# A transformer block pair with a product-key expert layer: order, pacing and engines of the row gathers and of the gate tables' one-hots

## The chip, the cores and the metric
One core of a Trainium2 chip runs the whole kernel. The metric is the device time of one execution in microseconds; the median of several runs is given. TensorE (PE in the profile, its weight loads PEld), VectorE (DVE), ScalarE (ACT), GpSimd (POOL) and SyncE (SP, which here only starts DMAs) each work through their own list of instructions in order and wait on semaphores.

## The reference
256 tokens of width 1024 go through two attention layers with feed-forward parts, a token mixer, a cross attention, and at the end an expert layer (`peer`). Only that last layer bears on the change:

```python
q = (xt @ w_pq).reshape(T, 8, 2, 128)
s = einsum('thpd,hpnd->thpn', q, subkeys)        # 2 x 128 scores per head
...                                              # top 16 of 128 twice, top 16 of their 256 sums
gate = softmax(best_s)                           # 8 heads x 16 experts per token
act = gelu(einsum('thkd,td->thk', peer_u[expert], xb)) * gate
out = einsum('thk,thkd->td', act, peer_v[expert])
```

`peer_u` and `peer_v` are tables of 16384 rows (128 x 128) of 1024 floats. Each token picks 128 rows of each.

## The kernel before
`phase_peer` splits the tokens. The first 192 (`TD`) are worked out **densely** on TensorE: all 16384 activations are formed, column by column (128 columns `j` of 128 experts), and multiplied with a gate table that is nearly all zeros. The last 64 tokens (`TS`) are worked out by **gathering** their rows: with two halves of the picks on the 128 partitions there are 64 indirect transfers of 128 rows from the `u` table and 64 from the `v` table, 512 KB each.

- **Column loop u** (L1589 to L1607): `whole` brings 512 KB of `u` per column in one of ten buffers, eight float32 matmuls make the column's scores (L1593, two TensorE instructions each in the trace), `ev_u` (L1537) applies Gelu on ScalarE (L1541, L1544) and, for tokens whose gate table is there already, multiplies it in on VectorE (L1542). In the first 71 columns the top-16 routing of both token groups is spread over the columns. `gather` (L1391) ends a group's routing and writes the transposed picks into the tables `IT`, `JT`, `GT` (L1417 to L1419).
- **Gate tables** (`gates`, L1514): from column `J0` = 75 on, `pump` (L1549) spreads 192 tokens over the matmuls. A token's 128 x 128 gate table is the product of two one-hot matrices (L1526): `oi` (`onehot`, L1500, four tokens at a time; three of the four on ScalarE as Abs and Relu, L1504 and L1505, the fourth on VectorE, L1506), made a group of four ahead, and `oj` times the gate (`weighed`, L1509, VectorE, L1511), made three tokens ahead in four buffers. After four tokens VectorE multiplies the table into the finished columns of `A` (L1531) and ScalarE copies the rest (L1533).
- **Column loop v** (L1639): `column` (L1620) brings 512 KB of `v` per column. Seven of eight columns are split into `hi` and `lo` parts (`granule`, L204: ScalarE L211, VectorE L212; `raw` has four buffers, `hi` and `lo` three each), as is the column of `A` (`split`, L268, L270 and L271), and cost 16 TensorE instructions (L1636, L1637); every eighth is used whole in float32 (L1634), also 16 instructions. Loop v adds up into eight PSUM banks. The last four columns stand apart (L1652) so that the final normalisation can start bank by bank.
- **Rows** (`gathered`, L1428): a generator that starts one transfer on GpSimd's queue per step (L1451). `beat[0]` is the newest column matmul; the transfer gets a semaphore wait on it. A transfer's use (`take`, L1433) is emitted when three later transfers have been started: for `u` VectorE multiplies with the token and adds up (L1438), for `v` it adds the row times its weight into `sacc` (L1446). `row` has four buffers. `Pace` (L1556) hands out the steps: 80 over the last 116 columns of loop u, 54 over 110 columns of loop v (L1586, L1587). `take` has no order of its own towards TensorE.

All instructions are emitted in Python's order, and the framework orders each engine's list from that by priority and by when operands and buffers come free; `granule` gives the split of a `v` column a lead of 80 instructions (L210, L1291). A dependency of class `Sync` is a semaphore wait on the chip; one of class `NoSync` only puts an instruction behind another when the lists are made.

Of the kernel before, what the change touches and what calls it, by code (L numbers as in the profile page):

```python
# [9 lines left out]
F32 = mybir.dt.float32  # L10
# [4 lines left out]
AF = mybir.ActivationFunctionType  # L15
OP = mybir.AluOpType
# [1269 lines left out]
def phase_peer(k, pool, wpool, out):  # L1286

    nc, I = k.nc, k.I
    mm = nc.tensor.matmul
    V = nc.vector  # L1290
    k.lead = 80  # L1291
    TS = 64
    TD = T - TS
# [18 lines left out]
    def slot(n, w):  # L1312
        return slots[:, n * 256:n * 256 + w]

    iota = wpool.tile([128, 128], F32, name="iota", bufs=1)
    nc.sync.dma_start(iota, I["consts"][:, CCOL["iota"]:CCOL["iota"] + 128])
    IT = wpool.tile([128, TD], F32, name="IT", bufs=1)
    JT = wpool.tile([128, TD], F32, name="JT", bufs=1)
    GT = wpool.tile([128, TD], F32, name="GT", bufs=1)

    es = wpool.tile([128, 64], I32, name="es", bufs=1)
    gs = wpool.tile([128, 64], F32, name="gs", bufs=1)
    hs = wpool.tile([128, 64], F32, name="hs", bufs=1)
    ws = wpool.tile([128, 64], F32, name="ws", bufs=1)
    x2 = wpool.tile([128, D], F32, name="x2", bufs=1)
# [65 lines left out]
    def gather(tt):  # L1391
        ri, rj, bv = picks[tt]

        mx = k.small.tile([128, 8], F32, name="pmx", bufs=2)
        V.tensor_reduce(mx, bv, AX.X, OP.max)
        V.tensor_tensor(bv, bv, mx[:, :, None].to_broadcast([128, 8, 16]), OP.subtract)
        nc.scalar.activation(bv, bv, AF.Exp)
        V.tensor_reduce(mx, bv, AX.X, OP.add)
        rc = k.small.tile([128, 8], F32, name="prc", bufs=2)
        V.reciprocal(rc, mx)  # L1400
        V.tensor_tensor(bv, bv, rc[:, :, None].to_broadcast([128, 8, 16]), OP.mult)
        ri, rj, bv = (t.rearrange("p a r -> p (a r)") for t in (ri, rj, bv))
        if tt == 1:

            own = slice(S0, 128)
            e = slot(8, 64).bitcast(I32)
            V.scalar_tensor_tensor(e[own], ri[own, 0:64], 128.0, rj[own, 0:64], op0=OP.mult, op1=OP.add)
            V.scalar_tensor_tensor(es[own], ri[own, 64:128], 128.0, rj[own, 64:128], op0=OP.mult, op1=OP.add)
            nc.sync.dma_start(es[0:S0], e[own])
            nc.sync.dma_start(gs[0:S0], bv[own, 0:64])  # L1410
            nc.sync.dma_start(gs[own], bv[own, 64:128])
        ps = k.tp()
        for n, src in enumerate((ri, rj, bv)):
            nc.tensor.transpose(ps[:, n * 128:n * 128 + 128], src, k.ident)
        w = min(128, TD - tt * 128)
        s = slice(tt * 128, tt * 128 + w)
        V.tensor_scalar(IT[:, s], ps[:, 0:w], -1.0, None, op0=OP.mult)  # L1417
        V.tensor_copy(JT[:, s], ps[:, 128:128 + w])
        V.tensor_copy(GT[:, s], ps[:, 256:256 + w])  # L1419
        yield  # L1420

    def routing(tt):
        for h in range(0, 8, 2):
            yield from interleave([route(h + i, tt) for i in range(2)])
        yield from gather(tt)


    def gathered():  # L1428
        AHEAD = 3
        todo = []  # L1430
        sacc = None

        def take():  # L1433
            nonlocal sacc
            kind, c, r = todo.pop(0)
            col = slice(c, c + 1)
            if kind == "u":
                V.scalar_tensor_tensor(r, r, 1.0, x2, op0=OP.mult, op1=OP.mult, accum_out=hs[:, col])  # L1438
                if c == 63:
                    nc.scalar.activation(ws, hs, AF.Gelu)  # L1440
                    V.tensor_tensor(ws, ws, gs, OP.mult)
            elif c == 0:
                sacc = wpool.tile([128, D], F32, name="x2", bufs=1)
                V.tensor_scalar(sacc, r, ws[:, col], None, op0=OP.mult)
            else:
                V.scalar_tensor_tensor(sacc, r, ws[:, col], sacc, op0=OP.mult, op1=OP.add)  # L1446

        for kind, table in (("u", urow), ("v", vrow)):
            for c in range(64):
                r = wpool.tile([128, D], F32, name="row", bufs=4)  # L1450
                i = nc.gpsimd.indirect_dma_start(out=r, out_offset=None, in_=table,  # L1451
                                                 in_offset=bass.IndirectOffsetOnAxis(ap=es[:, c:c + 1], axis=0))

                k.tc.add_manual_dep(i.ins, beat[0].ins.name, mybir.DependencyInfo(
                    mybir.DependencyClass.Sync, mybir.DependencyReason.DATA), reason="pace")
                todo.append((kind, c, r))
                if len(todo) > AHEAD:
                    take()
                yield
        while todo:  # L1460
            take()
            yield
        low = wpool.tile([128, D], F32, name="row", bufs=4)
        nc.sync.dma_start(low[S0:128], sacc[0:S0])
        x = k.x[S0:128, 1, :]
        V.tensor_tensor(x, x, sacc[S0:128], OP.add)
        yield
        V.tensor_tensor(x, x, low[S0:128], OP.add)
        yield

    J0 = 75
# [13 lines left out]
    def whole(j, ap):  # L1485

        name, bufs = (("raw", 4), ("hi", 3), ("raw", 4), ("lo", 3))[j % 4]
        raw = k.ring.tile([128, 1024], F32, name=name, bufs=bufs)
        nc.sync.dma_start(raw, ap)
        return raw  # L1490

    beat = [None]
# [7 lines left out]
    def onehot(t0):  # L1500

        oi = wpool.tile([128, 4, 128], F32, name="oi", bufs=2)
        for u in range(3):
            nc.scalar.activation(oi[:, u], iota, AF.Abs, bias=IT[:, t0 + u:t0 + u + 1])  # L1504
        nc.scalar.activation(oi[:, 0:3], oi[:, 0:3], AF.Relu, bias=k.one_col, scale=-1.0)  # L1505
        V.tensor_scalar(oi[:, 3], iota, IT[:, t0 + 3:t0 + 4], 0.0, op0=OP.add, op1=OP.is_equal)  # L1506
        return oi

    def weighed(t):  # L1509
        oj = wpool.tile([128, 128], F32, name="oj", bufs=4)  # L1510
        V.tensor_scalar(oj, iota, JT[:, t:t + 1], GT[:, t:t + 1], op0=OP.is_equal, op1=OP.mult)  # L1511
        return oj

    def gates():  # L1514
# [22 lines left out]
    def ev_u(j, ps):  # L1537
        n = done
        if n:
            g = wpool.tile([128, TD], F32, name="ge", bufs=2)  # L1540
            nc.scalar.activation(g[:, :n], ps[:, :n], AF.Gelu)  # L1541
            V.tensor_tensor(A[:, j, :n], A[:, j, :n], g[:, :n], OP.mult)  # L1542
        if n < TD:
            nc.scalar.activation(A[:, j, n:], ps[:, n:], AF.Gelu)  # L1544
# [4 lines left out]
    def pump():  # L1549
        nonlocal slot_no, emitted  # L1550
        slot_no += 1
        while emitted < TD * slot_no / (8 * (128 - J0) - 16):
            next(tables, None)
            emitted += 1
# [18 lines left out]
    for c in range(8):  # L1573
        ps = k.tp()
        nc.tensor.transpose(ps[:, 0:128], xn[0][:, c * 128:c * 128 + 128], k.ident)
        nc.tensor.transpose(ps[:, 128:TD], xn[1][0:S0, c * 128:c * 128 + 128], k.ident[0:S0, 0:S0])
        col = k.gains[:, GCOL["peer"] + c:GCOL["peer"] + c + 1]
# [5 lines left out]
    FIRST = 12  # L1583
    routes = [Pace(early, 16, FIRST), Pace(late, 29, J0 - 4 - FIRST)]
    rows = gathered()
    rows_u = Pace(rows, 80, 128 - FIRST)  # L1586
    rows_v = Pace(rows, 54, 110)  # L1587

    for j in range(128):  # L1589
        w = whole(j, I["u"][j])  # L1590
        ps = k.acc()
        for c in range(8):
            beat[0] = mm(ps[:, :TD], w[:, c * 128:c * 128 + 128], xf[:, c], start=c == 0, stop=c == 7)  # L1593
            if j >= J0:
                pump()
        ev_u(j, ps[:, :TD])
        cols = j + 1
        if j < FIRST:
            routes[0]()
        elif j < J0 - 4:  # L1600
            routes[1]()
        if j == FIRST - 1:
            routes[0].rest()
        if j == J0 - 5:
            routes[1].rest()
        if j >= FIRST:
            rows_u()  # L1607
    for _ in tables:
        pass

# [72 lines left out]
    s = k.small.tile([128, 2], F32, name="ss", bufs=2)  # L1683
    V.tensor_tensor(s, ss[:, 0], ss[:, 1], OP.add)
    inv = k.rsqrt(s, 2, 1.0 / D)
    for tt in range(2):
        nc.scalar.activation(y[:, tt, 0:512], z[:, tt, 0:512], AF.Copy, scale=inv[:, tt:tt + 1])
        V.tensor_scalar(y[:, tt, 512:1024], z[:, tt, 512:1024], inv[:, tt:tt + 1], None, op0=OP.mult)
        for nb in range(2):
            n = slice(nb * 512, nb * 512 + 512)  # L1690
# [3 lines left out]
def body(tc, I, out, upto=None):  # L1694
# [6 lines left out]
    with ExitStack() as root:  # L1701
# [25 lines left out]
        if "peer" in todo:  # L1727
            with ExitStack() as c:
                phase_peer(k, *pools(c, "peer", "p", "w"), out)
        else:  # L1730
            for tt in range(2):
                nc.sync.dma_start(out[0, tt * 128:tt * 128 + 128, :], k.x[:, tt, :])
# [15 lines left out]
```

## Time and profile before

| | us |
|---|---|
| median of 3 runs (lowest, highest) | 1837.44 (1831.9, 1841.64) |
| the profiled execution | 1830.55 |
| its span, first to last instruction | 1828.8 |
| TensorE busy in the span | 1757.9 (96%) |
| VectorE / ScalarE busy | 1213.9 (66%) / 871.9 (48%) |

The columns of loop u run from about 1061 us to 1458 us of the span, with gate tables from about 1267 us; loop v follows to about 1815 us. Busy time of TensorE is that of overlapping instructions, so a stretch at 100% can be at its peak or not; where the pace matters, instructions per microsecond are counted. The sum of the prediction is made against the 1830.55 us of the profiled execution.

### The profile page before, as it was taken

The numbers are of one execution on the slowest core, as the hardware profiler recorded it, in microseconds if no ns is written. First come the engines' busy times: TensorE is split into PE (matmuls) and PEld (weight loads), VectorE is DVE, ScalarE is ACT, GpSimd is POOL, SyncE is SP. The second block draws the span as 40 slices with busy tenths as digits, with TensorE's granted clock in tenths as the row PEclk, the third lists the DMA queues.
The fourth block names the chain that finished last, engine by engine and source line by source line (L and its number), as shares of the span: only waits on it lengthen the run. The fifth ranks groups of instructions, "written<-read, shape, count | busy, mean of one in ns | idle before, by whom it ended". The sixth has DMA issues, their size and how long they took to land.

```text
span 1828.8 us, 30479 instructions
## 1 busy us (share of the span) xinstructions
PE 1757.9 (96%) x11606; PEld 1642.5 (90%) x11606; DVE 1213.9 (66%) x2486; ACT 871.9 (48%) x1737; POOL 192.1 (11%) x184
## 2 busy tenths in 40 slices
PE   8999999999999999999999999999999988888897
PEld 7889998888899879988788999999999888888897
DVE  6867675688677566744475886775677766666665
ACT  6655544555544457765454521113555534343443
POOL 2000000000000001220000002222111122211200
PEclk9999999999999999999999999999999999999999
DMA  7435555643565656322463478999777688787864
GB/s 243 124 121 184 179 184 191 191 133 108 174 183 184 189 192 197 127 92 81 151 214 121 162 241 308 326 336 326 243 236 234 199 274 281 269 282 265 289 220 137
DMA packets 105363, 374.47 MB, mean 205 GB/s; under 512 B 12385, under 2 KB 14081, under 8 KB 104833
## 3 DMA queue, kind: packets, MB, share of 16 engines
q1 hardware_dynamic: 86080, 303.31, 50.8%
q0 software_dynamic: 19136, 69.21, 10.6%
q8 instruction: 92, 1.51, 0.3%
q14 instruction: 55, 0.44, 0.1%
HBM read 368.20 MB, written 3.15 MB: 203 GB/s over the span
## 4 chain that ended last, share of the span: by engine, by line
PE 69%; issue 14%; DMA 7%; DVE 5%; POOL 2%; ACT 2%; POOLq 0%; SPq 0%; ACTq 0%; DVEq 0%
PE acc L217 15%; PE acc L219 15%; PE acc L218 14%; PE acc L1593 13%; DMA row<-in_v,es 4%; DMA row<-in_urow,es 3%; POOL row L1451 2%; DVE lo L212 2%; PE tp L1144 1%; PE tp L1526 1%; ACT hi L211 1%; PE tp L395 1%; PE tp L325 1%; PE tp L407 1%; PE tp L402 1%
## 5 line engine op out<-in xcount | busy, mean ns | idle before, releaser
L211 ACT CAST hi<-raw 128x1024 fp32r<-128x1024 f32 (+2 forms) x420 | 436.4, 1039 | 562.8 <-PE acc L219 159.4
L212 DVE TENSOR_TENSOR lo<-raw,hi 128x1024 fp32r<-128x1024 f32 (+2 forms) x420 | 512.7, 1221 | 247.5 <-ACT hi L211 243.7
L217 PE MATMUL acc<-xal,hi 128*128 128x256 f32 x1272 | 365.6, 287 | 0.8 <-ACT hi L211 0.8
L219 PE MATMUL acc<-xah,lo 128*128 128x256 f32 x1272 | 361.7, 285 | 0.5 <-DVE lo L212 0.5
L218 PE MATMUL acc<-xah,hi 128*128 128x256 f32 x1272 | 361.8, 285 | 0.0
L217 PEld LDWEIGHTS acc<-xal,hi 128*128 128x128 f32 x1272 | 244.8, 192 | 2.8 <-ACT hi L211 1.2
L219 PEld LDWEIGHTS acc<-xah,lo 128*128 128x128 f32 x1272 | 244.5, 192 | 1.2 <-DVE lo L212 0.8
L218 PEld LDWEIGHTS acc<-xah,hi 128*128 128x128 f32 x1272 | 244.9, 193 | 0.6 <-issue 0.2
L1593 PE MATMUL acc<-xf,raw 128*128 128x192 f32 x1024 | 193.3, 328 | 0.0
L1593 PEld LDWEIGHTS acc<-xf,raw 128*128 128x128 f32 x1024 | 167.4, 192 | 0.1
L1446 DVE SCALAR_TENSOR_TENSOR x<-row,ws,x 128x1024 f32<-128x1024 f32 x63 | 80.8, 1283 | 99.9 <-DMA row<-in_v,es 99.9
L1438 DVE SCALAR_TENSOR_TENSOR row<-row,x 128x1024 f32<-128x1024 f32 x64 | 78.2, 1221 | 85.6 <-DMA row<-in_urow,es 85.4
L1451 POOL DMA_INDIRECT row<-in_v,es x64 | 70.9, 1108 | 288.1 <-PE acc L1637 150.7
L1593 PE MATMUL acc<-xf,hi 128*128 128x192 f32 x512 | 96.4, 327 | 0.0
L1451 POOL DMA_INDIRECT row<-in_urow,es x64 | 65.3, 1020 | 296.4 <-PE tp L1360 88.9
L1593 PE MATMUL acc<-xf,lo 128*128 128x192 f32 x512 | 95.8, 327 | 0.0
L1544 ACT ACTIVATE A<-acc 128x192 f32<-128x192 f32 (+25 forms) x125 | 36.8, 298 | 113.4 <-PE acc L1593 112.9
L1526 PE MATMUL tp<-oj,oi 128*128 128x128 f32 x384 | 76.1, 280 | 10.7 <-DVE oj L1511 9.9
L1636 PE MATMUL tp<-xah,hi 128*128 128x384 f32 x252 | 83.1, 379 | 0.0
L1593 PEld LDWEIGHTS acc<-xf,hi 128*128 128x128 f32 x512 | 82.9, 191 | 0.1
L1593 PEld LDWEIGHTS acc<-xf,lo 128*128 128x128 f32 x512 | 82.8, 191 | 0.1
L1526 PEld LDWEIGHTS tp<-oj,oi 128*128 128x128 f32 x384 | 66.2, 190 | 16.8 <-DVE oj L1511 12.1
(477 smaller groups left out, 3574.1 us busy)
## 6 DMA issues: line engine op xcount, KB each, us to landing
raw<-in_v SPq DMA_DIRECT2D x128, 512.0 KB, 4.7
raw<-in_u SPq DMA_DIRECT2D x64, 512.0 KB, 4.8
raw<-in_gate SPq DMA_DIRECT2D x44, 512.0 KB, 3.6
raw<-in_up SPq DMA_DIRECT2D x44, 512.0 KB, 3.6
raw<-in_down SPq DMA_DIRECT2D x44, 512.0 KB, 3.6
hi<-in_u SPq DMA_DIRECT2D x32, 512.0 KB, 4.7
lo<-in_u SPq DMA_DIRECT2D x32, 512.0 KB, 5.1
raw<-in_gates SPq DMA_DIRECT2D x16, 512.0 KB, 3.5
```

The costliest lines, as they stand in the source:

```text
L211: nc.scalar.copy(hi[:, :w], raw[:, :w])
L212: nc.vector.tensor_tensor(lo[:, :w], raw[:, :w], hi.bitcast(F32)[:, :w], OP.subtract)
L217: mm(ps, ah, bl, start=start, stop=False)
L218: mm(ps, ah, bh, start=False, stop=False)
L219: mm(ps, al, bh, start=False, stop=stop)
L1438: V.scalar_tensor_tensor(r, r, 1.0, x2, op0=OP.mult, op1=OP.mult, accum_out=hs[:, col])
L1446: V.scalar_tensor_tensor(sacc, r, ws[:, col], sacc, op0=OP.mult, op1=OP.add)
L1451: i = nc.gpsimd.indirect_dma_start(out=r, out_offset=None, in_=table, in_offset=bass.IndirectOffsetOnAxis(ap=es[:, c:c + 1], axis=0))
L1526: mm(ps[:, u * 128:u * 128 + 128], oi[:, u], ojs.pop(0), start=True, stop=True)
L1544: nc.scalar.activation(A[:, j, n:], ps[:, n:], AF.Gelu)
L1593: beat[0] = mm(ps[:, :TD], w[:, c * 128:c * 128 + 128], xf[:, c], start=c == 0, stop=c == 7)
L1636: mm(acc[c][:, 0:2 * TD], vh[:, s], m, start=j == 0, stop=False)
```

## The change
Rows: a use of a row gets a `NoSync` dependency on `beat[0]`, the column matmul that is newest when the third later transfer is started; the transfer keeps its `Sync` dependency (a helper, `behind`, makes both). Pacing: 38 steps over columns 12 to 74 and 48 over columns 75 to 127 of loop u, 48 over 112 columns of loop v. One-hots: `oi` of four tokens is one VectorE comparison of 128 x 512; three of four `oj` are made by ScalarE in two instructions (Abs, then Relu with the gate as bias and its negative as scale), every fourth by VectorE as before. `gather` writes `IT` without a sign, and by ScalarE the negatives `NJT` and `NGT`.

```diff
-        V.tensor_scalar(IT[:, s], ps[:, 0:w], -1.0, None, op0=OP.mult)
-        V.tensor_copy(JT[:, s], ps[:, 128:128 + w])
-        V.tensor_copy(GT[:, s], ps[:, 256:256 + w])
+        for n, (t, m) in enumerate(((IT, None), (JT, NJT), (GT, NGT))):
+            V.tensor_copy(t[:, s], ps[:, n * 128:n * 128 + w])
+            if m is not None:
+                nc.scalar.activation(m[:, s], ps[:, n * 128:n * 128 + w], AF.Copy, scale=-1.0)
...
+        def behind(i, how):
+            k.tc.add_manual_dep(i.ins, beat[0].ins.name, mybir.DependencyInfo(how, mybir.DependencyReason.DATA),
+                                reason="pace")
...
             if kind == "u":
-                V.scalar_tensor_tensor(r, r, 1.0, x2, op0=OP.mult, op1=OP.mult, accum_out=hs[:, col])
-                if c == 63:
-                    nc.scalar.activation(ws, hs, AF.Gelu)
-                    V.tensor_tensor(ws, ws, gs, OP.mult)
+                i = V.scalar_tensor_tensor(r, r, 1.0, x2, op0=OP.mult, op1=OP.mult, accum_out=hs[:, col])
...
+            behind(i, mybir.DependencyClass.NoSync)
+            if (kind, c) == ("u", 63):
+                nc.scalar.activation(ws, hs, AF.Gelu)
+                V.tensor_tensor(ws, ws, gs, OP.mult)
...
-                k.tc.add_manual_dep(i.ins, beat[0].ins.name, mybir.DependencyInfo(
-                    mybir.DependencyClass.Sync, mybir.DependencyReason.DATA), reason="pace")
+                behind(i, mybir.DependencyClass.Sync)
...
         oi = wpool.tile([128, 4, 128], F32, name="oi", bufs=2)
-        for u in range(3):
-            nc.scalar.activation(oi[:, u], iota, AF.Abs, bias=IT[:, t0 + u:t0 + u + 1])
-        nc.scalar.activation(oi[:, 0:3], oi[:, 0:3], AF.Relu, bias=k.one_col, scale=-1.0)
-        V.tensor_scalar(oi[:, 3], iota, IT[:, t0 + 3:t0 + 4], 0.0, op0=OP.add, op1=OP.is_equal)
+        V.tensor_tensor(oi, iota[:, None, :].to_broadcast([128, 4, 128]),
+                        IT[:, t0:t0 + 4, None].to_broadcast([128, 4, 128]), OP.is_equal)
         return oi
...
-        V.tensor_scalar(oj, iota, JT[:, t:t + 1], GT[:, t:t + 1], op0=OP.is_equal, op1=OP.mult)
+        if t % 4 == 0:
+            V.tensor_scalar(oj, iota, JT[:, t:t + 1], GT[:, t:t + 1], op0=OP.is_equal, op1=OP.mult)
+        else:
+            nc.scalar.activation(oj, iota, AF.Abs, bias=NJT[:, t:t + 1])
+            nc.scalar.activation(oj, oj, AF.Relu, bias=GT[:, t:t + 1], scale=NGT[:, t:t + 1])
         return oj
...
-    rows_u = Pace(rows, 80, 128 - FIRST)
-    rows_v = Pace(rows, 54, 110)
+    rows_early = Pace(rows, 38, J0 - FIRST)
+    rows_late = Pace(rows, 48, 128 - J0)
+    rows_v = Pace(rows, 48, 112)
...
-        if j >= FIRST:
-            rows_u()
+        if j >= J0:
+            rows_late()
+        elif j >= FIRST:
+            rows_early()
```

## Rows read from the trace of the kernel before

**Rows 1.** Page: busy us (share of the span) xinstructions by engine
```profile
PE 1757.9 (96%) x11606; PEld 1642.5 (90%) x11606; DVE 1213.9 (66%) x2486; ACT 871.9 (48%) x1737; POOL 192.1 (11%) x184
```

**Rows 2.** Windows, us: PE, PEld, DVE, ACT, POOL busy (instructions), clock, DMA share, GB/s
```profile
1250.00:1458.00 208.00, 197.25 (x1304) 191.14 (x1303) 145.07 (x410) 104.51 (x349) 38.17 (x39) 1.00 0.71 239
1458.00:1740.00 282.00, 248.24 (x1593) 242.14 (x1592) 186.26 (x233) 114.40 (x185) 57.09 (x50) 0.96 0.81 278
```

**Rows 3.** Windows of 20 us: a full one of loop u, one disturbed and one full of loop v
```profile
1220.00:1240.00 20.00, 20.00 (x125) 20.00 (x125) 17.54 (x56) 5.35 (x13) 5.60 (x5) 1.00 0.93 342
...
1580.00:1600.00 20.00, 18.51 (x106) 18.26 (x107) 12.40 (x16) 5.19 (x8) 3.78 (x3) 0.83 0.61 201
...
1780.00:1800.00 20.00, 20.00 (x141) 20.00 (x139) 10.92 (x13) 9.04 (x13) 0.00 (x0) 1.00 0.69 223
```

**Rows 4.** Waits (us in total, times, longest), 1458 to 1740
```profile
PEld tp L1637 <- DVE lo L212: 39.7, 23, 4.0
...
DVE x L1446 <- DMA row<-in_v,es: 86.3, 37, 6.6
...
ACT hi L211 <- DMA raw<-in_v: 87.8, 39, 4.5
```

**Rows 5.** Chain that ended last, one round of it in loop v
```profile
1494.87 7.28 DMA row<-in_v,es
...
1503.45 1.23 DVE lo L212
```

**Rows 6.** Tile row, whole span, then tile raw, 1470 to 1735
```profile
DMA to landing us min/median/max: 4.1/5.9/9.0
...
DMA to landing us min/median/max: 3.4/4.9/8.7
```

**Rows 7.** Groups by line, 1560 to 1829: VectorE and ScalarE work of a loop v column
```profile
L212 DVE TENSOR_TENSOR lo<-raw,hi 128x1024 fp32r<-128x1024 f32 x80 | 97.6, 1221 | 32.2 <-ACT hi L211 32.2
L211 ACT CAST hi<-raw 128x1024 fp32r<-128x1024 f32 x79 | 82.8, 1049 | 147.5 <-PE acc L1636 68.5 <-DMA raw<-in_v 50.6 <-DVE x L1446 11.9
L1446 DVE SCALAR_TENSOR_TENSOR x<-row,ws,x 128x1024 f32<-128x1024 f32 x32 | 41.0, 1282 | 58.8 <-DMA row<-in_v,es 58.8
L271 DVE TENSOR_TENSOR xah<-A,xah 128x192 fp32r<-128x192 f32 x42 | 14.7, 351 | 0.0
```

**Rows 8.** Waits, 1250 to 1458: weight loads and VectorE
```profile
PEld tp L1526 <- DVE oj L1511: 12.1, 17, 1.8
...
DVE row L1438 <- DMA row<-in_urow,es: 39.1, 25, 4.5
DVE x L1446 <- DMA row<-in_v,es: 13.6, 10, 2.9
```

**Rows 9.** Timeline: one token's two instructions, four of the column's, the next token's
```profile
1301.87 0.39 PE L1526 MATMUL tp<-oj,oi 128*128 128x128 f32 x2
...
1302.09 0.82 PE L1593 MATMUL acc<-xf,raw 128*128 128x192 f32 x4
...
1302.74 0.38 PE L1526 MATMUL tp<-oj,oi 128*128 128x128 f32 x2
```

**Rows 10.** Groups by line, 1267 to 1458 (last row: 1000 to 1100)
```profile
L1511 DVE TENSOR_SCALAR oj<-iota,JT,GT 128x128 f32<-128x128 f32 x188 | 57.6, 347 | 4.5 <-PE tp L1526 4.1
L1506 DVE TENSOR_SCALAR oi<-iota,IT 128x128 f32<-128x128 f32 x46 | 13.0, 282 | 0.0
L1531 DVE TENSOR_TENSOR A<-A,tp 128x300 f32<-128x300 f32 (+46 forms) x47 | 26.5, 563 | 2.6 <-PE tp L1526 1.8 <-issue 0.5
...
L1504 ACT ACTIVATE oi<-iota,IT 128x128 f32<-128x128 f32 x138 | 46.6, 393 | 29.9 <-PE tp L1526 29.9
L1505 ACT ACTIVATE oi<-oi,one_col 128x384 f32<-128x384 f32 x46 | 28.3, 616 | 0.7
L1533 ACT COPY A<-tp 128x212 f32<-128x212 f32 (+46 forms) x47 | 11.8, 250 | 45.5 <-DVE A L1531 45.1
...
L1384 DVE TENSOR_TENSOR A<-A,iota 128x512 f32<-128x512 f32 x8 | 5.4, 679 | 0.3 <-ACT A L1381 0.3
```

More of the change, by code (lines that the diff above doesn't have):

```diff
@@ L1316, in phase_peer @@
     nc.sync.dma_start(iota, I["consts"][:, CCOL["iota"]:CCOL["iota"] + 128])
-    IT = wpool.tile([128, TD], F32, name="IT", bufs=1)
-    JT = wpool.tile([128, TD], F32, name="JT", bufs=1)
-    GT = wpool.tile([128, TD], F32, name="GT", bufs=1)
+    IT, JT, GT, NJT, NGT = (wpool.tile([128, TD], F32, name=n, bufs=1) for n in ("IT", "JT", "GT", "NJT", "NGT"))
     es = wpool.tile([128, 64], I32, name="es", bufs=1)
@@ L1437, in take @@
             if kind == "u":
-                V.scalar_tensor_tensor(r, r, 1.0, x2, op0=OP.mult, op1=OP.mult, accum_out=hs[:, col])
-                if c == 63:
-                    nc.scalar.activation(ws, hs, AF.Gelu)
-                    V.tensor_tensor(ws, ws, gs, OP.mult)
+                i = V.scalar_tensor_tensor(r, r, 1.0, x2, op0=OP.mult, op1=OP.mult, accum_out=hs[:, col])
             elif c == 0:
                 sacc = wpool.tile([128, D], F32, name="x2", bufs=1)
-                V.tensor_scalar(sacc, r, ws[:, col], None, op0=OP.mult)
+                i = V.tensor_scalar(sacc, r, ws[:, col], None, op0=OP.mult)
             else:
-                V.scalar_tensor_tensor(sacc, r, ws[:, col], sacc, op0=OP.mult, op1=OP.add)
+                i = V.scalar_tensor_tensor(sacc, r, ws[:, col], sacc, op0=OP.mult, op1=OP.add)
+            behind(i, mybir.DependencyClass.NoSync)
+            if (kind, c) == ("u", 63):
+                nc.scalar.activation(ws, hs, AF.Gelu)
+                V.tensor_tensor(ws, ws, gs, OP.mult)
         for kind, table in (("u", urow), ("v", vrow)):
```

## The prediction

> **What bounds the kernel now.** I read the page first: TensorE is busy 96% of the span [rows 1], so only its gaps and its pace can give time, and any other engine matters through them. Then the windows of the last layer. In the gate-table part of loop u weight loads, whose gaps show waiting better than the overlapping matmuls do, are busy 191.1 of 208 us, and in loop v up to the last row transfer 242.1 of 282 us [rows 2]. In loop u ahead of the gate tables TensorE is full (first row of [rows 3]); nothing is to be had there. The reader should next count instructions instead of busy time: once the rows are done loop v passes 141 instructions in 20 us (last row of [rows 3]); a column has 16, so a column takes 16 x 20/141 = 2.27 us. With rows, 1593 instructions, 99.6 columns, take 282 us: 2.83 us each [rows 2]. At the full pace they would take 226 us, so the rows cost loop v **56 us**. Of these, weight loads wait 39.7 us for `lo` on VectorE [rows 4]; much of the rest is clock: one disturbed slice has a granted clock of 0.83, where undisturbed ones have 1.00 [rows 3].
>
> Why is VectorE late? Its work fills 186 of 282 us, but it stands 86.3 us more in front of a row that has not landed, 37 times, up to 6.6 us [rows 2, 4], and those two make 272 of 282. The chain shows one round: a row takes 7.28 us from issue, then comes the row operation, `lo` behind it, then TensorE [rows 5]. TensorE's column releases the next transfer, so this is a loop that sets the pace. ScalarE's 87.8 us in front of `raw` [rows 4] hang on it: a `raw` buffer is free for its next load only when `lo` has read it.
>
> Why does VectorE ask so early? In program order a use stands three transfers behind its own, 3 x 110/54 = 6.1 columns. But VectorE splits as far ahead of TensorE as three `lo` buffers allow, three columns. That leaves 3.1 columns x 2.83 = 8.8 us between start and use at best, against landings of 4.1 to 9.0 us [rows 6] that begin only after the semaphore and the queue.
>
> **The change, part by part.**
>
> *Order of the row operations, loop v.* No instruction is added. A use now stands in VectorE's list behind what was listed when the column of the third later transfer was; the splits with their lead of 80 come first. The distance becomes 3 x 112/48 = 7 columns of TensorE's own count. Even if VectorE runs three columns ahead of it, 4 x 2.27 = 9.1 us remain, and if it doesn't, 15.9 us; the longest landing is 9.0 [rows 6]. So the 86 us of waits go almost wholly. No semaphore is added, so nothing new queues on VectorE; what comes later is the release of `row`, and GpSimd's transfer n+4 waits for use n. Use n stands behind column n+3 and the transfer has its own wait 2.33 columns, 5.3 us, further on, while a row operation takes 1.28 us [rows 7]: GpSimd's queue is not held unless VectorE lags by 4 us. SyncE's queue is passed by nothing.
>
> What is late next in loop v? VectorE per column: 7/8 x (1.221 + 0.351) = 1.38 us, and 42 row operations left (128 less 38 and 48) over 128 columns, 0.33 x 1.28 = 0.42: 1.80 of 2.27 us [rows 7]. ScalarE 7/8 x (1.05 + 0.35) = 1.2. Transfers: (128 + 42) x 0.524 MB in 128 x 2.27 us is 307 GB/s; loop u keeps 342 GB/s with TensorE full [rows 3]. All fit, but at 79% VectorE still delays some `lo` by a row operation, and the change-over from loop u stays. I keep a fifth of the loss: **-44 us**, between -56 (all) and -28 (half, first rival). Beyond 1740 us no row is left; I take nothing there.
>
> *Pacing.* 0.60 instead of 0.69 steps per column ahead of the gate tables, 0.91 instead of 0.69 beside them, 48 instead of 54 in loop v, for the longer columns. Ahead of them TensorE is full either way: 0 us, covered by that fullness, and if the cover failed the transfers, fewer than now, would not be the cause. Beside the gate tables VectorE gets 48 instead of 0.69 x 53 = 36.6 operations of 1.3 us: +15 us of its work. In loop v the six fewer transfers are in the -44.
>
> *Gate tables.* A token's two instructions with half a column's float32 work take 0.87 us from one token to the next [rows 9], of which the four column instructions at 20/125 us [rows 3] are 0.64, leaving 0.11 each. The stretch of 208 us holds 384 such and 920 column instructions: 42 + 147 = 189 to 192 us, so 16 to 19 us are lost, in line with the 16.9 us that weight loads are not busy [rows 2]. 12.1 of them wait for `oj` on VectorE [rows 8], which stands 39.1 + 13.6 us before rows. Those waits go as in loop v: at 0.91 steps per column three transfers are 3.3 columns of about 3.5 us.
>
> The engines change places. VectorE, 48 groups of four tokens: `oi` 0.68 instead of 0.28 us (the nearest row is a comparison of two broadcast operands of the same size, 679 ns) = +19 us; `oj` loses 144 x 0.347 = -50 [rows 10]; with the rows +15. Net -16 of work and -52 of waits: ample. ScalarE loses 48 x (3 x 0.393 + 0.616) = 86 us and gets 144 x 2 x 0.393 = 113: +27 on 104.5, 131 of some 190 us, or 2.7 of 3.9 us per group. The second instruction has scale and bias from SBUF; no row shows two such operands, so its price is bounded by 0.393 (one) below and 0.616 (three times the width) above, at most +32 us more; I take the lower, the same width. The Trainium skill (ScalarE: Activation LUTs, section What ACT_TABLE_LOAD costs) puts about 93 ns on each operand read that way; by it the second costs 0.48 us, 13 us more in all, still under the stretch. The same page (Rules for kernel authors) says relu, add and multiply belong on VectorE, not ScalarE, which speaks against this part; row for row it is right (0.79 for 0.347 us), and it decides only if ScalarE becomes late, the third rival. I take half of the loss: **-8 us**, between -16 and +10.
>
> *`gather`.* Four more ScalarE copies of under 0.25 us (L1533 in [rows 10]) where ScalarE is busy 5 of 20 us [rows 3]: 0.
>
> **Sum.** 1830.6 - 44 - 8 = 1778.6 us against the profiled execution. That one lies below the lowest of the three runs and 6.9 us under their median; the median is what is asked, so I add the 6.9: **1785 us**. A measurement of this kernel can tell about 0.5%, 9 us, from no change.
>
> **Rivals.**
> 1. *The `raw` ring comes late next.* A round of one buffer is landing 4.9 (up to 8.7) [rows 6] + 1.05 + 1.22 + a row operation in front 1.28 = 8.5 us; four buffers give 4 x 2.27 = 9.1, but the whole column of every eight holds one until TensorE is through, and three give 6.8. Up to 1.7 us once or twice per eight columns, 16 to 32 times: about 28 us of the 44 are not got, **1813 us**. For it: ScalarE's 87.8 us before `raw` [rows 4]. Against: the full pace at the end has the same ring and whole columns, though at 223 GB/s [rows 3].
> 2. *The order does nothing*: the dependency asks for no wait, and if the lists come out as before, loop v keeps its 2.83 us. Six fewer rows give 6 x 56/47 = 7 us (47 rows in the stretch), the one-hots some 3: **1827 us**. Against: VectorE's early use needs it to be listed ahead of TensorE's column, which is what the edge forbids.
> 3. *ScalarE's queue becomes the loop, and the kernel slower.* ScalarE waits for VectorE's L1531 before L1533, 45 us now [rows 10], and `oj` would stand behind. If three tokens of lead don't cover it, a group takes in a row: a token's matmuls 0.3, a row operation 1.28, L1531 0.56, L1533 0.25, six instructions 2.36, two Gelus 0.5 = 5.2 us instead of 190/48 = 4.0: +60 us, **1845 us** with loop v's gain. It decides from the point where wait and six instructions exceed the 3.5 us of four tokens; against it, the `oj` of every fourth token stays on VectorE and the next three exist when L1533 waits.
>
> **Chances.** Forecast 0.70 (own range 1768 to 1802); first rival 0.14; second 0.08; third 0.08, of which a part, a few tens of us lost beside the gain of loop v, still ends faster. Faster by over 0.5%: 0.70 + 0.14 + 0.03 + 0.02 = 0.89; within 0.5%: 0.05; slower: 0.06. For 8 in 10 the range goes from 1766 (nearly all of 56 + 16 gone) to 1814, the first rival.
>
> **What would show it.** In the changed kernel: VectorE's wait for rows in loop v under 15 us; weight loads waiting for `lo` under 10 us; a column near 2.35 us and the clock 1.00 in nearly all slices of loop v; beside the gate tables weight loads waiting under 10 us, ScalarE busy about 130 us there. Wrong if rows still hold VectorE tens of us (second), if ScalarE waits for `raw` and TensorE for `hi` or `lo` (first), or if TensorE waits tens of us for `oj` from ScalarE (third).

## The result and the profile after

The changed kernel takes 1776.9 us (median of 4 runs, 1773.07 to 1780.63) against 1839.05 us: ratio 0.9668, 95% interval 0.9632 to 0.9704. The profiled execution took 1773.07 us, its span 1771.3 us. The prediction was faster, 1785 us within 1766 to 1814.

The page of the changed kernel, busy time by engine, answers to [rows 1]:

```profile
PE 1739.0 (98%) x11606; PEld 1632.8 (92%) x11606; DVE 1198.1 (68%) x2342; ACT 912.4 (52%) x1837; POOL 220.1 (12%) x184
```

The waits of its loop v, 1450 to 1761 us (engine, line, what it waited for; us in total, times, longest), answer to [rows 4]; weight loads, VectorE, ScalarE:

```profile
PEld tp L1648 <- DVE lo L212: 7.5, 9, 3.0
PEld tp L1647 <- ACT hi L211: 0.9, 2, 0.5
...
DVE lo L212 <- ACT hi L211: 77.7, 65, 4.6
...
DVE x L1473 <- DMA row<-x: 3.5, 1, 3.5
...
ACT hi L211 <- DMA raw<-in_v: 88.5, 48, 6.0
```

VectorE's 86.3 us in front of gathered rows are gone to nothing, weight loads wait 7.5 us for `lo` where they waited 39.7, and the one wait for a `row` that is left is another one, L1473, a transfer of the kernel's own sum. ScalarE still stands 88.5 us in front of `raw`, as long as before: ScalarE has time to spare, and the loop has become faster by 44.5 us with that wait unchanged.

Windows of the changed kernel (us; PE, PEld, DVE, ACT, POOL busy with instructions, clock, DMA share, GB/s), the gate tables, loop v, and three slices, answer to [rows 2, 3]:

```profile
1267.00:1450.00 183.00, 180.73 (x1231) 180.14 (x1230) 138.25 (x278) 143.33 (x449) 59.73 (x48) 1.00 0.82 279
1450.00:1760.00 310.00, 304.37 (x2059) 301.34 (x2058) 220.68 (x275) 142.21 (x220) 63.20 (x43) 0.99 0.81 285
...
1580.00:1600.00 20.00, 19.95 (x139) 19.65 (x137) 14.97 (x18) 8.95 (x14) 4.44 (x4) 1.00 0.90 317
1700.00:1720.00 20.00, 17.25 (x106) 16.99 (x106) 10.01 (x13) 7.42 (x11) 0.00 (x0) 0.91 0.62 198
1720.00:1740.00 20.00, 20.00 (x138) 20.00 (x137) 11.19 (x14) 8.99 (x14) 0.00 (x0) 1.00 0.66 219
```

Over the stretch with rows loop v passed 113 instructions in 20 us before (1593 in 282 us); now it passes 133 over its whole length (2059 in 310 us), and 138 to 140 in its undisturbed slices, rows beside it or not. Counted from the first matmul of a part to the first of the next, the time came from two places (in the kernel before loop v starts at 1463.5 us, not at 1458):

| us | before | after | difference |
|---|---|---|---|
| loop u up to the first gate table | 207.1 | 207.0 | -0.1 |
| gate tables to loop v | 196.4 | 183.0 | -13.4 |
| loop v, first to last matmul of a split column | 354.7 | 310.2 | -44.5 |
| from there to the end | 10.6 | 10.6 | 0 |

### The profile page after: what moved, and what is told of

Its sections match the earlier page's. It is cut to its first block, busy times and chain, and to the rows that moved or that the text cites. A ratio compares the mean times of both kernels' runs of the same rounds, so it can differ in the third digit from the quotient of the medians.

```text
span 1771.3 us, 30381 instructions
## 1 busy us (share of the span) xinstructions
PE 1739.0 (98%) x11606; PEld 1632.8 (92%) x11606; DVE 1198.1 (68%) x2342; ACT 912.4 (52%) x1837; POOL 220.1 (12%) x184
## 4 chain that ended last, share of the span: by engine, by line
PE 83%; issue 6%; DMA 4%; DVE 4%; ACT 2%; POOL 0%; ACTq 0%; POOLq 0%; SPq 0%; DVEq 0%
PE acc L1602 18%; PE acc L217 15%; PE acc L219 15%; PE acc L218 15%; DMA raw<-in_v 4%; PE acc L1647 3%; PE tp L1647 2%; PE tp L1534 2%; PE tp L1144 1%; PE tp L1648 1%; PE acc L1648 1%; DVE lo L212 1%; ACT hi L211 1%; PE tp L395 1%; PE tp L325 1%
## 5 line engine op out<-in xcount | busy, mean ns | idle before, releaser
L1602 PE MATMUL acc<-xf,raw 128*128 128x192 f32 x1024 | 193.3, 328 | 0.0
L1457 POOL DMA_INDIRECT row<-in_v,es x64 | 92.1, 1439 | 224.0 <-PE acc L1648 81.0
L1457 POOL DMA_INDIRECT row<-in_urow,es x64 | 72.0, 1125 | 278.9 <-PE acc L1602 120.0
L1647 PE MATMUL acc<-xah,hi 128*128 128x384 f32 x252 | 79.1, 367 | 0.0
```

Of the source, the lines that this page charges most:

```text
L1647: mm(acc[c][:, 0:2 * TD], vh[:, s], m, start=j == 0, stop=False)
```

## The experiments

The theory: it is the **order** of the row operations in VectorE's list that frees TensorE, by the distance that it puts between a transfer and its use; pace and one-hots add little. Rivals: the sparser pace, the one-hots, the traffic of the transfers.

One measurement goes through all runs: the n-th start of a transfer (L1451 in the kernel before) and the n-th start of a use are paired, and the median of the difference over the last 48 transfers, most of them released in loop v, is the **lag**. Beside it stands the **list distance**: in the order in which VectorE works, how many columns behind the column that releases a transfer the last split in front of its use is (median over the transfers released in loop v; columns count from 0). The releasing column follows from the pace, and the trace agrees: transfer 30 of the kernel before is released by column 28, whose last matmul ends at 1544.09 us, and it starts at 1544.36. "us" is the median of each kernel's runs. The ratios below are each against runs of the kernel before beside the experiment, whose medians were 1832.0 to 1835.8 us.

| kernel | list distance | lag us | row waits in loop v | `lo` waits there | gate tables | loop v | us |
|---|---|---|---|---|---|---|---|
| before | 3 | 6.5 | 86.3 | 42.2 | 196.4 | 354.7 | 1839.1 |
| e1 (no order) | 3 | 5.8 | 91.1 | 42.0 | 193.3 | 355.5 | 1828.9 |
| e9 (before, written one on) | 3 | 6.9 | 99.9 | 49.6 | 198.1 | 368.8 | 1839.1 |
| e5 (order, one on) | 5 | 7.4 | 41.9 | 16.4 | 196.3 | 319.0 | 1797.6 |
| e5b (order, two on) | 7 | 11.6 | 0.5 | 4.0 | 180.8 | 303.6 | 1767.8 |
| e2 (order alone) | 8 | 15.7 | 0 | 6.1 | 180.2 | 308.3 | 1768.5 |
| after | 9 | 17.3 | 0 | 7.5 | 183.0 | 310.2 | 1776.9 |

**e1: the change without its order.**

```diff
-            behind(i, mybir.DependencyClass.NoSync)
```

> The changed kernel without the order of the row operations (pace and one-hots as changed). Theory (the order is what frees loop v): VectorE waits 70 us or more for rows in loop v again, weight loads wait 30 us or more for lo, and the time is 1815 to 1830 us. Rival (the pace, with six rows fewer in loop v and even spacing, does most of it): under 30 us of row waits in loop v, and 1775 to 1795 us.

1828.89 us, ratio to the kernel before 0.9972 (0.995 to 0.9995). Of the 3.3% only 0.3% is left. VectorE's waits in its loop v, 1458 to 1813 us, are those of before:

```profile
DVE x L1447 <- DMA row<-in_v,es: 91.1, 33, 6.7
DVE lo L212 <- ACT hi L211: 39.0, 38, 3.4
```

The new pace and the new one-hots together are worth next to nothing while the order is missing.

**e2: the order alone**, on the kernel before, with its old pace and one-hots.

```diff
-                V.scalar_tensor_tensor(sacc, r, ws[:, col], sacc, op0=OP.mult, op1=OP.add)
+                i = V.scalar_tensor_tensor(sacc, r, ws[:, col], sacc, op0=OP.mult, op1=OP.add)
+            behind(i, mybir.DependencyClass.NoSync)
```

(and so for the other uses; `behind` is the helper of the change)

> The kernel before with the order alone (old pace, old one-hots). Theory: row waits on VectorE in loop v under 10 us, 42 to 46 us gained there, and beside the gate tables about half of the 13 us that the whole change gained: 1783 to 1793 us. Rival (the order only works together with the sparser pace, since 3 x 2.04 columns are shorter): 30 us or more of row waits stay in loop v and the time is above 1800 us.

1768.46 us, ratio 0.9651 (0.9617 to 0.9684): the whole gain, and 15 us under the range that I expected. What I had missed is the gate tables: they take 180.2 us with no wait of TensorE at all, so that the row waits were the whole of the loss there too, not half. Two windows of e2's loop v:

```profile
1480.00:1500.00 20.00, 20.00 (x141) 20.00 (x140) 16.53 (x21) 7.93 (x13) 4.17 (x4) 1.00 0.94 340
1500.00:1660.00 160.00, 159.35 (x1087) 158.89 (x1085) 126.18 (x152) 77.86 (x121) 42.47 (x34) 1.00 0.93 334
```

With the old pace and all its transfers, at 334 to 340 GB/s, TensorE passes 136 to 141 instructions in 20 us. This also rules out that the traffic of the transfers slowed loop v: there is more of it per microsecond here than in the kernel before (278 GB/s [rows 2]).

**e3: the change with the old one-hots.**

```diff
-        V.tensor_tensor(oi, iota[:, None, :].to_broadcast([128, 4, 128]),
-                        IT[:, t0:t0 + 4, None].to_broadcast([128, 4, 128]), OP.is_equal)
+        for u in range(3):
+            nc.scalar.activation(oi[:, u], iota, AF.Abs, bias=IT[:, t0 + u:t0 + u + 1])
...
-        if t % 4 == 0:
...
+        V.tensor_scalar(oj, iota, JT[:, t:t + 1], GT[:, t:t + 1], op0=OP.is_equal, op1=OP.mult)
```

> The changed kernel with the one-hots as before. Theory (one-hots matter only beside the gate tables, and there less than the order): 1777 to 1786 us, TensorE waiting for oj on VectorE again up to 10 us beside the gate tables, loop v unchanged. Rival (with 48 row operations there VectorE can't carry the one-hots, so that the move to ScalarE was needed): TensorE waits 15 us or more for oj, 1787 to 1797 us.

1773.56 us, ratio 0.9676 (0.964 to 0.9713), where the change has 0.9668. TensorE waits for nothing from VectorE there. So the exchange of engines bought nothing: VectorE at 48 row operations beside the gate tables carries the old one-hots. That it costs nothing either, though ScalarE's work grew, fits with both engines being under 80% busy there in the changed kernel (138.25 and 143.33 of 183 us).

**e4: the change with the old pace.**

```diff
-    rows_early = Pace(rows, 38, J0 - FIRST)
-    rows_late = Pace(rows, 48, 128 - J0)
-    rows_v = Pace(rows, 48, 112)
+    rows_u = Pace(rows, 80, 128 - FIRST)
+    rows_v = Pace(rows, 54, 110)
...
```

> The changed kernel with the old pace (80 steps over loop u, 54 over 110 columns of loop v). Theory (with the order in place the pace hardly matters, six more row operations of 1.28 us lie beside TensorE's work): 1774 to 1784 us, no row waits in loop v. Rival (a shorter distance of 6.1 columns or the fuller loop v brings waits back): 20 us or more of waits for rows or lo in loop v, 1790 to 1805 us.

1770.05 us, ratio 0.9661 (0.9627 to 0.9694), lag 15.7 us, no row waits. The pace is not needed.

**e5 and e5b: one and two transfers on instead of three.**

```diff
-        AHEAD = 3
+        AHEAD = 1
```

(e5b: 2)

> The changed kernel with a use ordered behind the column one transfer on instead of three. Theory (it is the distance in TensorE's columns that must exceed the landing): 2.33 columns of 2.27 us are 5.3 us, with the 1.4 us by which uses lie behind that in the changed kernel 6.7, against landings of 4.1 to 9.0 us and the queue in front: 20 to 70 us of row waits in loop v and 1792 to 1822 us. Rival (any order towards TensorE is enough, because it only stops VectorE from running ahead): under 10 us of row waits, 1770 to 1782 us.

> The changed kernel with a use ordered behind the column two transfers on. Theory (distance): 4.67 columns are 10.6 us, with 1.4 more 12, over the longest landing: under 8 us of row waits, 1772 to 1783 us, the same as three transfers on. Rival (three are needed): above 1787 us.

1797.62 us, ratio 0.9819 (0.9777 to 0.986), and 1767.82 us, 0.9653 (0.9614 to 0.9692). The time answers to the distance as the theory says: at a lag of 7.4 us, within the landings of e5's own rows, 4.2 to 9.7 us, half of the row waits come back; at 11.6 us, over e5b's longest landing of 9.5, 0.5 us of them is left. Any order is not enough, and three transfers on is more than is needed. (e3, e4 and e5b came out 3 to 4 us under the ranges that I had set for them.) The waits in e5's loop v, 1461 to 1720 us:

```profile
DVE x L1447 <- DMA row<-in_v,es: 41.9, 21, 5.3
```

**e9: the kernel before, a use written one transfer on, no order.** This asks where an unordered use comes to stand.

```diff
-        AHEAD = 3
+        AHEAD = 1
```

> The kernel before, with a use written one transfer behind its own instead of three, and no order. Theory (without an order the lists hold a use one column behind its transfer, wherever it is written): the lists, the 80 to 90 us of row waits in loop v and the time stay, 1825 to 1842 us. Rival (the prediction's account: a use stands where it is written, 6.1 columns on, less a lead of three): written 2.04 columns on it would come four columns or 9 us earlier for each of 48 transfers, row waits in loop v go above 200 us and the time above 1900 us.

1839.05 us, ratio 1.0023 (0.999 to 1.0057): the same time. The lists show why. For four transfers of loop v, the column whose end releases the transfer, the column at whose end its use is written, and the last split in front of the use in VectorE's list:

```
transfer        30            31            32            33
before      28, 34, 32    30, 36, 33    32, 38, 35    34, 40, 38
e9          28, 30, 32    30, 32, 33    32, 34, 35    34, 36, 38
after       18, 25, 27    21, 28, 31    23, 30, 32    25, 32, 34
```

Without an order the framework puts a use three or four columns behind its transfer's release, not the one that I expected, but as expected at the same distance whether it was written two columns on (e9), six (before) or seven (e1); with the order it stands two or three columns behind the place where it was written. In the trace of the kernel before VectorE comes to the use 0.7 to 7.6 us after the start of its transfer (median 4.8, last 48 transfers), and waits there until the row has landed. Why the framework chooses this place was not tried.

**e6: a use that needs no row.** The `v` uses of the kernel before read a tile that is there already; the gathered `v` rows are fetched and left out of the sum.

```diff
-                V.scalar_tensor_tensor(sacc, r, ws[:, col], sacc, op0=OP.mult, op1=OP.add)
+                V.scalar_tensor_tensor(sacc, k.x[:, 0, :], ws[:, col], sacc, op0=OP.mult, op1=OP.add)
```

> The kernel before, where the v row operations read a tile that is there already instead of the row: transfers, operations and lists of other work stay, the wait for the row goes. It leaves out the use of the gathered v rows. Theory (it is the wait on VectorE, not the transfers and not the operations, that costs loop v its time): loop v takes 308 to 316 us instead of 354.7, and the kernel 1785 to 1797 us (the u rows' waits beside the gate tables stay). Rival (the transfers' traffic delays the columns' own loads): loop v stays above 335 us.

1814.3 us, the median of three runs (1809.3 to 1817.1; a fourth took 6030.6), ratio 0.9886 (0.9838 to 0.9934), and loop v 337.0 us: a miss, and by its number the rival's. But the experiment did not keep what it was to keep: with no transfer to wait for, the 64 uses were lifted to the stretch from 1393 to 1535 us, up to 187 us ahead of their transfers, and from 1470 us on VectorE worked through them with little else between. Two windows of it, the first in that stretch, the second behind it (this execution's clock shows 0.95 where TensorE is full and less where it waits):

```profile
1500.00:1520.00 20.00, 15.95 (x89) 15.27 (x88) 19.82 (x21) 5.21 (x9) 2.09 (x2) 0.83 0.51 175
...
1560.00:1580.00 20.00, 20.00 (x139) 20.00 (x138) 10.09 (x14) 9.67 (x15) 4.84 (x5) 0.95 0.97 343
```

In the first VectorE is busy 19.82 of 20 us and TensorE passes 89 instructions. In the second the rows are still being fetched, at 343 GB/s and a DMA share of 0.97, and TensorE passes 139. So here too the traffic of the transfers is not what slowed loop v; as a measure of the wait alone the run is spoilt.

**e8: the last transfer's addition, later.** In the changed kernel the slice from 1700 us has 106 instructions and a clock of 0.91. VectorE there (start us, us, operation, idle time before it and its releaser):

```profile
1698.02 1.22 DVE L1471 TENSOR_TENSOR x<-x,x 64x1024 f32<-64x1024 f32 x1
1699.27 0.36 DVE L271 TENSOR_TENSOR xah<-A,xah 128x192 fp32r<-128x192 f32 x1
1703.11 1.22 DVE L1473 TENSOR_TENSOR x<-x,row 64x1024 f32<-64x1024 f32 x1 [3.47 <-DMA row<-x]
1704.36 1.23 DVE L212 TENSOR_TENSOR lo<-raw,hi 128x1024 fp32r<-128x1024 f32 x1
```

The same wait shows once more, with the transfer that moves half of the gathered sum to the other partitions: its use stands too early in the list, `lo` behind it, TensorE behind that. e8 is e2 with

```diff
         V.tensor_tensor(x, x, sacc[S0:128], OP.add)
         yield
-        V.tensor_tensor(x, x, low[S0:128], OP.add)
+        yield
+        yield
+        behind(V.tensor_tensor(x, x, low[S0:128], OP.add), mybir.DependencyClass.NoSync)
...
-    rows_v = Pace(rows, 54, 110)
+    rows_v = Pace(rows, 56, 114)
```

> The kernel before with the order alone, and the last addition of the gathered part put six columns behind its transfer, also ordered behind TensorE's column. Theory (the dip near 1700 us is the same fault once more: VectorE waits 3.5 us for one 256 KB transfer, TensorE 3 us for lo, and its clock dips): 4 to 6 us under the order alone, 1762 to 1765 us, without a window of clock below 1.00 in the last 100 us of loop v. Rival (the splits behind it had slack, the dip comes from the end of the rows): 1767 to 1771 us.

1764.38 us, ratio 0.9622 (0.9593 to 0.9651); 0.9651 for e2 lies at the edge of that interval, so the 4 us are likely and not shown. In the trace the wait is gone and the slice is whole, though another, 1620 to 1640 us, has 112 instructions at a clock of 0.91:

```profile
1700.00:1720.00 20.00, 20.00 (x141) 20.00 (x139) 12.55 (x17) 10.41 (x16) 0.00 (x0) 1.00 0.76 258
```

**The changed kernel and e8 side by side**, on one chip:

> The changed kernel again, for comparison on one chip. Theory (the new pace and the one-hots add nothing to the order): 4 to 13 us above the next kernel. Rival (they help): below it.

> The order alone with the late addition again, for comparison on one chip: 1760 to 1768 us, and its interval apart from that of the changed kernel. Rival: the two can't be told apart.

1773.25 us (six runs, 1769.92 to 1779.32), 0.9664 (0.9619 to 0.9708), against 1765.44 us (six runs, 1762.96 to 1769.5), 0.9623 (0.958 to 0.9666). The intervals against the kernel before overlap, the runs themselves do not: every run of e8 was faster than every run of the change. The order with the late addition, and without new pace or one-hots, is faster than the change by about 8 us. In the profiled executions part of that is in the gate tables, 187.0 us in this run of the change, whose clock from 1440 to 1460 us is 0.86, and 180.2 in e8's. Weight loads of the change there, and its ScalarE:

```profile
PEld tp L1534 <- ACT oj L1519: 4.0, 1, 4.0
```

```profile
ACT hi L211 <- DMA raw<-in_v: 5.6, 2, 4.4
```

At the change-over to loop v ScalarE stands in front of the first `raw` of loop v with an `oj` behind it in its queue. It is seen in the change (2.5 and 4.0 us) and, with the old `oi` on ScalarE, in e3 (2.5 us); not in e2, e4 and e8, which have the old pace, and in e5b, with the new pace and two transfers on, the worst is 0.6 us. Whether the new pace brings it on, and why, was not tried further and stays open.

## Why the prediction was right, point by point

- **What bounds the kernel: right.** The loss was counted as 56 us in loop v and 16 to 19 us beside the gate tables. Loop v fell by 44.5 us and the gate tables by 13.4, in e2 by 46.4 and 16.2. One step was wrong: ScalarE's 87.8 us in front of `raw` do not hang on the rows, they are 88.5 us after.
- **Order in loop v, -44 us: right in mechanism, in size partly by luck.** 44.5 us; row waits 0 where under 15 were asked for, weight loads waiting for `lo` 7.5 us where under 10 were. A column takes 310.2/128 = 2.42 us instead of the 2.35 named; in its undisturbed slices 16 x 20/139 = 2.30. The clock is below 1.00 in one slice only, the one of e8. e1, e2, e5 and e5b show that it is the order, and its distance. The luck: at 2.27 us a column all of loop v would take 290.6 us, so that 64 us were lost before and not 56 (beyond 1740 us, where I took nothing, the slice to 1760 passed 104 instructions at a clock of 0.83), and of these nearly 20 are still lost, not 12.
- **Why VectorE asks early: wrong.** "A use stands three transfers behind its own, 3 x 110/54 = 6.1 columns", less a lead of three, "leaves 3.1 columns x 2.83 = 8.8 us". The use was written there, but it did not stand there: the list held it three columns behind the release, where e2, with the same place in the program and the order, has eight; and the lag was 6.5 us. The number came near by chance. By this account e9 would have been slower by far, and it was the same. The distance after, 7 columns or 15.9 us if VectorE does not lead, was near: the use is written 7 columns on and stands 9 on in the list, and 17.3 us were measured.
- **Gate tables, -8 us: too small.** 13.4 us, and 16.2 with the order alone. Of the loss there I kept half for a ScalarE that might be late; apart from the change-over it was not. Groups of the changed kernel, 1250 to 1440 us, answer to [rows 10]:

```profile
L1519 ACT ACTIVATE oj<-oj,GT,NGT 128x128 f32<-128x128 f32 x140 | 68.4, 493 | 3.6
L1518 ACT ACTIVATE oj<-iota,NJT 128x128 f32<-128x128 f32 x141 | 56.0, 399 | 23.4 <-PE tp L1534 22.9 <-PE acc L1602 0.5
...
L1508 DVE TENSOR_TENSOR oi<-iota,IT 128x512 f32<-128x512 f32 x48 | 32.9, 686 | 0.0
```

  The comparison of 128 x 512 costs 0.686 us, as its neighbour's row said (0.679). The instruction with two operands per partition costs 0.493 us, not the lower bound of 0.393 that I took. The estimate from the Trainium skill (ScalarE: Activation LUTs, What ACT_TABLE_LOAD costs) was 0.48 us, and the trace agrees with it within 3%. ScalarE was busy 143.3 of 183 us instead of the 131 named. The Trainium skill's rule that such work belongs on VectorE (ScalarE: Activation LUTs, Rules for kernel authors) agrees with the trace instruction by instruction, 0.89 for 0.35 us, and with the experiments in that the move gained nothing.
- **Pacing, 0 us: right** (e1, e4), but for the stall at the change-over.
- **From the profiled execution to the median, +6.9 us: too much.** The change's median is 3.8 us above its profiled execution. Against the profiled executions the sum was 52 us and the measured difference 1830.55 - 1773.07 = 57.5; the rest of the distance from 1785 to 1776.9 is this term.
- **The rivals.** The `raw` ring came late in one slice, not as a loop: from 1480 to 1500 us ScalarE waits up to 6.0 us for `raw`, TensorE passes 118 instructions, and 3 us are lost, where the rival had 28. Elsewhere ScalarE and VectorE wait for `raw` and `hi` as long as before or longer, and TensorE hardly does. The order did do what it says. ScalarE's queue became late at one place, 2.5 to 4.0 us, not in a loop. (That rival's 1845 us has the gate tables' 8 us in it; with loop v's gain alone its sum is 1853.)

## What to carry to other kernels

A wait in front of a transfer on an engine that is 66% busy can set the pace of another engine that is 96% busy: look at what stands behind the waiting instruction in its list, and compare the time from the transfer's start to its use with the landing times. Where a list is made by priority, the place at which a use is written need not decide where it stands; an ordering dependency on the engine that sets the pace, put so many of its steps on that they exceed the longest landing, cost nothing here and was the whole of a 3% gain. Change one thing at a time where several are at hand: two of the three parts here did nothing.

## What the runs showed that was not expected

A use listed three columns behind its transfer's release held TensorE although VectorE had a third of its time free: 86 us of VectorE's waits cost 46 us of loop v (e2). Part of that is the clock: the kernel before has slices of loop v at 0.91 and 0.83 [rows 3], others with as many gaps at 1.00, and the average of its loop v is 0.96; e2 has 1.00 up to 1680 us. Loop v keeps its full pace at a DMA share of 0.97 (e6). ScalarE's waits for `raw`, 87.8 us before and 88.5 after, cost little in the changed kernel, 3 us in one slice.
